# Two-layer decoder trunk on one core: the modulation columns get other stages

## The chip, the core and the metric

The kernel runs on one core of a Trainium2 chip. The core has a matrix engine (TensorE, PE in the profile), a vector engine (VectorE, DVE), an activation engine (ScalarE, ACT), GpSimd (POOL) and a sync engine (SP) that here only issues DMAs. The metric is the device time of one execution in microseconds (us), the median of several runs. Everything is float32, and the matrix products are made of three products each (high by high, high by low, low by high), with each operand split into a rounded high part and the rest.

## The reference

A sequence of 512 tokens with 1024 features passes two layers. Layer 0 mixes tokens by retention, layer 1 by an mLSTM; each has four heads (256 wide for queries and keys, 512 for values) and is followed by a channel mixer with a causal convolution (2816 wide). What the change touches is the conditioning by the vector c:

```python
c_act = jax.nn.silu(c)
for i in range(DEPTH):
    mod = c_act @ ada_w[i] + ada_b[i]
    sh_t, sc_t, gt_t, sh_f, sc_f, gt_f = [m[:, None, :] for m in jnp.split(mod, 6, axis=-1)]
    h = rmsnorm(x, norm_tok_g[i]) * (1.0 + sc_t) + sh_t
    ...
    x = x + gt_t * y
    h = rmsnorm(x, norm_ffn_g[i]) * (1.0 + sc_f) + sh_f
    x = x + gt_f * conv_ffn(h, ffn_w_up[i], ffn_conv_w[i], ffn_conv_b[i], ffn_w_down[i])
return rmsnorm(x, final_g)
```

Each layer's `mod` has 6 times 1024 values: a shift, a scale and a gate for the token mixer and the same for the channel mixer. Features lie on 128 partitions, so a layer has 48 columns of 128 values and the trunk has 96.

## The kernel before

**A modulation column.** Line 456, `side_work`, computes one: SP loads the column's 128 rows of `ada` (1025 floats each, 512.5 KB) into a buffer `ada`, and VectorE multiplies it with the row c and sums along the row (line 452, `gemv`, one SCALAR_TENSOR_TENSOR over 128x1025). For a scale column a tiny instruction makes the gain from it (line 466). The buffers come from a ring of two (`KINDS`, key "a", line 48), so that a third column's load waits until the first one's product has run. The chunks of the down projections (line 510) use the same two buffers.

**When.** 16 columns (the shifts and scales of the first norm) are computed in the opening stage. The other 80 stand in the list `side` in the order of use (lines 1866 to 1874): 8 gates of the first mixer; 16 shifts and scales of the first channel mixer's norm, with its 8 gates behind them; the same 24 for the second layer's token mixer (16 and 8); 16 and 8 for the second channel mixer. `SIDES` (line 30) says how many are taken from the list in which named stage; they are spread evenly over the stage's items (lines 1884 to 1892). An item is a block of matrix products with one chunk of weights. `gate` is the first matmul from that item on: the column's load is not planned to be issued before it. This is an order in the plan and no wait on the chip.

**The stages.** `heads` (line 1295) writes the order of a mixer's four heads out by hand. Stage names are "ret" (retention) or "ml" (mLSTM) with q (queries and keys), v (values), g (gates), o (output projection) and the number of the head, 0 to 3; "o1" projects head 1's output, "o2" the first pieces of head 2's, and "last" the rest beside the coming norm (`boundary`, line 1045). Between them stand scores (S), attention (A) and the ends of heads. The order is q1, v1, g1, (o0), q2, v2, g2, q3, v3, g3, o1, o2, last. Then comes the channel mixer: "up0" or "up1" for its first products, "fold0" or "fold" for the long middle part, where products of the up projection and pieces of the down projection alternate, and "end0" or "end1" for the last group of the down projection beside the next norm. Stage "fold0" hands out its 32 columns by itself (line 891).

**The order on each engine.** `Plan` records every instruction and then orders each engine's own by a simulated run (line 258): an instruction has a price in us (lines 170 to 191), a due time that follows from the matmul which needs its result (lines 241 to 252), and among those that can start soonest the one with the earliest due time goes first. The columns have late due times, so they fill what the simulated VectorE has left over. The list of each engine is then fixed; on the chip an engine takes it strictly in order and waits by semaphore where an operand is missing. The price of a plain DMA is 2.45 us per MB (line 172), of an accumulating one 5.4. The accumulating DMAs are issued by POOL and make the low parts of weights (line 483); all weights are loaded by SP, on the same queue as the columns.

**PE's order** follows the items, with neighbours that interleave. The names of PE's outputs tell the stages: `p` (products of folded pairs, in q, g and fold), `pv` (values), `psc` (scores), `pav` (attention), `po` (output and down projections), `pf` and `pp` (products right behind a norm).

Of the kernel before, what the change touches and what calls it, by code (L numbers as in the profile page):

```python
# [26 lines left out]
GROUPS = [4, 4, 4, 4, 6]  # L27
WCOLS = 1024
WTILES = 18
SIDES = [('ret q1', 4), ('ret v1', 2), ('ret g1', 2), ('ret v3', 6), ('ret g3', 10), ('fold0', 32), ('ml v3', 4), ('ml g3', 8), ('ml o1', 4), ('up1', 8)]  # L30
O_ADDED = (2, 3)
FREE_STEPS = (0, 3)
VADDED = (1, 6, 5, 7, 3)
# [346 lines left out]
def trunk(ctx: ExitStack, tc: tile.TileContext, xT, cb, pos, vec, ident, decay, zmask, ada, w_s0, w_in0, w_v0,  # L380
# [957 lines left out]
    class Ffn:  # L1338
# [75 lines left out]
        def items(self, norm):  # L1414
# [4 lines left out]
            steps, run = folded(folds, self.h, self.start.sums.terms, pairs, downs,  # L1419
                                dict(SIDES).get(f"fold{self.layer}", 0))  # L1420
            now[0] = f"up{self.layer}"
# [456 lines left out]
    for n, (uses, fn, free) in enumerate(items):  # L1878
# [5 lines left out]
        same = [m for m, (used, _, _) in enumerate(items) if steps_at[m] == steps_at[n] and used]  # L1884
        quota = dict(SIDES).get(steps_at[n], 0)
        if not quota or n not in same:
# [121 lines left out]
```

## Time and profile before

| | |
|---|---|
| median of 3 runs | 1508.07 us (1507.39 to 1513.26) |
| the profiled execution | 1507.64 us |
| its span, first to last instruction | 1505.8 us |
| columns, bytes of each | 96, 512.5 KB |
| mean granted clock of TensorE | 0.993 |

Where the stages lie in the span, by the names of PE's outputs and counts of its matmuls (us): ret q1 87.5 to 126.8, v1 to 150.7, g1 to 177.5, o0 to 199.4, q2 to 221.0, v2 to 243.0, g2 to 270.3, q3 to 291.0, v3 to 310.5, g3 to 337.0, o1 to 367.2, o2 to 378.0, last with the norm to 435.0, up0 to 457.0, fold0 to 718.5, end0 to 752.0, the norm and head 0 of ml to 825.0, ml q1 to 854.3, v1 to 878.4, g1 to 907.5, o0 to 929.5, q2 to 951.0, v2 to 973.6, g2 to 1001.8, q3 to 1024.5, v3 to 1043.1, g3 to 1072.0, o1 to 1099.0, o2 to 1110.0, last with the norm to 1174.5, up1 to 1196.3, then the second fold and the end. Neighbouring stages interleave by some us.

A row of the view by stretches gives a stretch of the span (start and end, its length), then the busy time of PE, of PE's weight loads, of DVE, ACT and POOL with the number of instructions, then the granted clock of TensorE (1.00 is full), the mean busy share of the 16 DMA engines (it can pass 1 a little, as packets are counted where they start) and the GB/s that they moved. The stretch's length less PE's busy time is PE's idle time. In the timeline a bracket at the end gives the engine's idle time before the instruction and what ended it.

### The profile page before, as it was taken

To read this page: it belongs to the slowest core of one execution; us is meant where nothing else is said; L and a number is where in the kernel's file an instruction comes from. 1 tells how busy PE (TensorE), PEld (TensorE's weight loads), DVE (VectorE), ACT (ScalarE), POOL (GpSimd) and SP (SyncE) were. 2 spreads that over 40 slices of the span, in tenths; PEclk is the share of its full clock that TensorE was granted. 3 is DMA by queue.
4 is the path that set the end of the run, shared out by engine and by line. 5 is a ranking of instruction groups with operands and counts; after the bars stand their busy time and mean duration, and the time that the engine had idled before them with its cause. 6 is when DMAs were issued, how large, how long until landed. Compare 5 with 4: busy or idle time off the path is not lost.

```text
span 1505.8 us, 27268 instructions
## 1 busy us (share of the span) xinstructions
PE 1472.7 (98%) x10477; PEld 1375.8 (91%) x10477; DVE 1268.1 (84%) x2141; ACT 1070.0 (71%) x1601; POOL 283.5 (19%) x311
## 2 busy tenths in 40 slices
PE   9999999999999999999999999998999999999997
PEld 6889999988999989999989998998989989999997
DVE  6998979498988888898887987888989887777786
ACT  4558868776587676776679985998747867766752
POOL 0234232322011111110001322131211111111100
PEclk9989999999999999999999999999999999999999
DMA  9567978898688989999358866889796888876841
GB/s 362 173 161 191 278 172 215 213 298 233 183 222 210 269 224 273 264 250 270 106 158 194 193 188 141 192 199 225 237 288 161 224 235 215 205 194 166 199 132 57
DMA packets 92980, 315.00 MB, mean 209 GB/s; under 512 B 12193, under 2 KB 14625, under 8 KB 92850
## 3 DMA queue, kind: packets, MB, share of 16 engines
q0 software_dynamic: 31824, 115.88, 41.7%
q1 hardware_dynamic: 61026, 197.38, 36.9%
q8 instruction: 82, 1.34, 0.3%
q14 instruction: 48, 0.39, 0.1%
HBM read 195.23 MB, written 2.12 MB: 131 GB/s over the span
## 4 chain that ended last, share of the span: by engine, by line
PE 85%; DVE 6%; DMA 5%; ACT 2%; issue 2%; POOL 0%; SPq 0%; DVEq 0%; POOLq 0%; ACTq 0%
PE p L376 34%; PE po L376 24%; PE pv L376 7%; PE pp L376 5%; PE pav L376 4%; PE pf L376 4%; PE pst L376 3%; PE psc L376 2%; DMA ada<-ada 1%; DMA wlo<-ws 1%; DMA wb<-w_in 1%; PE pc L376 1%; ACT whi L376 1%; DVE ada L376 1%; DMA wb<-w_up 1%
## 5 line engine op out<-in xcount | busy, mean ns | idle before, releaser
L376 PE MATMUL p<-hh,whi 128*128 128x256 f32 (+1 forms) x994 | 276.3, 278 | 4.4 <-DVE mc L376 4.3
L376 PE MATMUL p<-hl,whi 128*128 128x256 f32 x992 | 276.0, 278 | 0.6 <-DVE hl L376 0.5
L376 PE MATMUL p<-hh,wlo 128*128 128x256 f32 x992 | 273.9, 278 | 0.0
L376 ACT ACTIVATE wlo<-whi 128x1024 fp32r<-128x1024 f32 x221 | 233.1, 1060 | 49.9 <-PE po L376 19.3
L376 PEld LDWEIGHTS p<-hh,whi 128*128 128x128 f32 x994 | 188.1, 189 | 5.3 <-DVE mc L376 4.5
L376 PEld LDWEIGHTS p<-hl,whi 128*128 128x128 f32 x992 | 187.8, 189 | 1.4 <-DVE hl L376 1.1
L376 PEld LDWEIGHTS p<-hh,wlo 128*128 128x128 f32 x992 | 187.0, 189 | 0.1
L376 PE MATMUL p<-t24h,whi 128*128 128x256 f32 x744 | 166.1, 280 | 5.1 <-DVE p L376 3.6
L376 PE MATMUL po<-ggh,wlo 128*128 128x512 f32 (+1 forms) x448 | 153.0, 343 | 1.1 <-DVE wlo L376 1.1
L376 PE MATMUL po<-ggh,whi 128*128 128x512 f32 (+1 forms) x448 | 152.5, 343 | 1.4 <-ACT whi L376 1.4
L376 PE MATMUL po<-ggl,whi 128*128 128x512 f32 (+1 forms) x448 | 153.2, 343 | 0.0
L376 DVE SCALAR_TENSOR_TENSOR x<-po,mod,x 128x512 f32<-128x512 f32 (+1 forms) x184 | 112.0, 625 | 37.7 <-PE po L376 37.2
L376 ACT CAST whi<-raw 128x1024 fp32r<-128x1024 f32 (+1 forms) x117 | 117.5, 1018 | 32.2 <-PE po L376 9.5
L376 PE MATMUL p<-t24l,whi 128*128 128x256 f32 x496 | 138.0, 278 | 0.0
L376 PEld LDWEIGHTS p<-t24h,whi 128*128 128x128 f32 x744 | 127.1, 189 | 8.3 <-DVE p L376 4.7
L376 DVE SCALAR_TENSOR_TENSOR ada<-ada,c_ext 128x1025 f32<-128x1025 f32 x96 | 121.5, 1268 | 9.8 <-DMA ada<-ada 9.7
L376 POOL DMA_DIRECT2D wlo<-wa x62 | 54.6, 880 | 382.2 <-ACT wlo L376 260.7
L376 PE MATMUL po<-yh,whi 128*128 128x256 f32 (+1 forms) x354 | 116.4, 330 | 0.6 <-DVE x L376 0.6
L376 PE MATMUL po<-yl,whi 128*128 128x256 f32 (+1 forms) x352 | 116.3, 330 | 0.3 <-DVE yl L376 0.2
L376 PE MATMUL po<-yh,wlo 128*128 128x256 f32 (+1 forms) x352 | 115.1, 329 | 0.0
L376 DVE SCALAR_TENSOR_TENSOR cv<-p,vecs,cv 128x510 f32<-128x510 f32 (+1 forms) x144 | 105.8, 742 | 7.5 <-ACT cv L376 7.2
L376 ACT CAST whi<-ws 128x1024 fp32r<-128x1024 f32 x86 | 90.2, 1051 | 28.4 <-DVE ws L376 18.7
(285 smaller groups left out, 4428.5 us busy)
## 6 DMA issues: line engine op xcount, KB each, us to landing
ada<-ada SPq DMA_DIRECT2D x96, 512.5 KB, 6.4
wlo<-ws POOLq DMA_DIRECT2D x73, 512.0 KB, 6.9
wlo<-wa POOLq DMA_DIRECT2D x62, 512.0 KB, 6.9
wlo<-wt POOLq DMA_DIRECT2D x44, 512.0 KB, 6.7
wlo<-raw POOLq DMA_DIRECT2D x36, 512.0 KB, 8.8
wa<-w_up SPq DMA_DIRECT2D x36, 512.0 KB, 6.8
wb<-w_up SPq DMA_DIRECT2D x36, 512.0 KB, 6.9
raw<-w_o SPq DMA_DIRECT2D x32, 512.0 KB, 8.8
```

Of the source, the lines that this page charges most:

```text
L376: getattr(c.obj, c.name)(*[real(v) for v in c.a], **{key: real(v) for key, v in c.k.items()})
```

## The change

The list `SIDES` gets other stages and numbers; the 80 columns keep their order, and nothing else changes.

```diff
-SIDES = [('ret q1', 4), ('ret v1', 2), ('ret g1', 2), ('ret v3', 6), ('ret g3', 10), ('fold0', 32), ('ml v3', 4), ('ml g3', 8), ('ml o1', 4), ('up1', 8)]
+SIDES = [("ret q1", 2), ("ret v1", 4), ("ret g1", 4), ("ret g2", 2), ("ret q3", 2), ("ret g3", 3), ("ret o1", 4), ("ret o2", 4), ("fold0", 32), ("end0", 2), ("ml q1", 1), ("ml v1", 4), ("ml g2", 2), ("ml g3", 6), ("ml o2", 4), ("up1", 4)]
```

By stage, the number of columns before and after:

| stage | before | after | | stage | before | after |
|---|---|---|---|---|---|---|
| ret q1 | 4 | 2 | | end0 | 0 | 2 |
| ret v1 | 2 | 4 | | ml q1 | 0 | 1 |
| ret g1 | 2 | 4 | | ml v1 | 0 | 4 |
| ret g2 | 0 | 2 | | ml g2 | 0 | 2 |
| ret q3 | 0 | 2 | | ml v3 | 4 | 0 |
| ret v3 | 6 | 0 | | ml g3 | 8 | 6 |
| ret g3 | 10 | 3 | | ml o1 | 4 | 0 |
| ret o1 | 0 | 4 | | ml o2 | 0 | 4 |
| ret o2 | 0 | 4 | | up1 | 8 | 4 |
| fold0 | 32 | 32 | | sum | 80 | 80 |

Since the plan is made by the simulated run over all instructions, other instructions can change their place in an engine's order too.

## The prediction

> **What bounds the kernel now.** I read the page first, then the busy times by stretch, the waits, the timelines of SP and VectorE where PE stood still, and the chain of waits there.
>
> ```profile
> PE 1472.7 (98%) x10477; PEld 1375.8 (91%) x10477; DVE 1268.1 (84%) x2141; ACT 1070.0 (71%) x1601; POOL 283.5 (19%) x311
> q0 software_dynamic: 31824, 115.88, 41.7%
> q1 hardware_dynamic: 61026, 197.38, 36.9%
> L376 DVE SCALAR_TENSOR_TENSOR ada<-ada,c_ext 128x1025 f32<-128x1025 f32 x96 | 121.5, 1268 | 9.8 <-DMA ada<-ada 9.7
> ```
>
> PE is the bound: of the span's 1505.8 us it is idle for 33.1. The change touches none of its matmuls, so it can only win or lose idle time and clock. One column costs VectorE 1.27 us. On the DMA engines, SP's queue moved 197.38 MB in 36.9% of 1505.8 = 555.6 us, 2.81 us per MB, so a column of 0.525 MB takes 1.48 us of all 16 engines. POOL's accumulating queue takes 41.7% of 1505.8 / 115.88 = 5.42 us per MB, 2.84 us for a tile of 0.524 MB. Now the stretches where PE loses time:
>
> ```profile
> 87.50:126.80 39.30, 36.47 (x241) 34.43 (x240) 36.08 (x60) 24.95 (x40) 13.49 (x14) 0.87 0.52 135
> 291.00:310.50 19.50, 19.11 (x163) 18.75 (x163) 12.66 (x21) 13.40 (x20) 5.80 (x6) 1.00 1.00 263
> 310.50:337.00 26.50, 24.19 (x195) 23.19 (x194) 24.99 (x35) 20.01 (x33) 8.29 (x12) 1.00 1.01 307
> 457.00:718.50 261.50, 260.17 (x1896) 243.62 (x1896) 231.57 (x392) 180.57 (x254) 34.52 (x40) 1.00 0.91 250
> 1024.50:1043.10 18.60, 18.31 (x153) 17.92 (x152) 15.90 (x25) 17.82 (x26) 2.58 (x3) 1.00 1.04 258
> 1043.10:1072.00 28.90, 24.57 (x191) 24.11 (x190) 23.97 (x38) 20.23 (x32) 3.00 (x5) 0.94 0.85 244
> 1099.00:1110.00 11.00, 9.97 (x44) 7.95 (x43) 8.67 (x14) 4.72 (x6) 2.98 (x3) 1.00 1.04 331
> 1110.00:1151.60 41.60, 40.64 (x315) 38.55 (x314) 40.35 (x81) 24.66 (x42) 5.18 (x6) 1.00 0.66 175
> 1196.30:1245.00 48.70, 45.75 (x349) 43.15 (x348) 40.57 (x68) 31.95 (x45) 5.83 (x7) 1.00 0.86 227
> ```
>
> Length less PE's busy time gives PE's idle time: 2.83 us in ret q1, 0.39 in ret v3, 2.31 in ret g3, 1.33 in all of fold0, 0.29 in ml v3, 4.33 in ml g3, 1.03 and 0.96 beside the last heads of ml, 2.95 where the second fold begins. In ml g3 the clock is 0.94 too, which is 0.06 x 28.9 = 1.7 us of PE's time. All of these but ret q1 and fold0 are stages from which columns go. The stages next to the fourth heads have DMA shares of 1.00 to 1.04: there the DMA engines are full.
>
> **The change part by part: what goes.** 29 of the 80 columns change stage. Most expensive is ml v3, 4 columns before and none after:
>
> ```profile
> 1025.06 2.62 SPq L376 DMA_DIRECT2D ada<-ada  x2
> 1029.51 14.82 DMA wb<-w_in
> 1044.46 0.69 DVE L376 TENSOR_TENSOR ws<-wb 128x512 f32<-128x512 f32 x1 [2.25 <-DMA wb<-w_in]
> PE p L376 <- DVE mc L376: 4.3, 1, 4.3
> 1047.70:1051.20 3.50, 3.41 (x16) 3.41 (x17) 3.50 (x7) 2.29 (x5) 0.86 (x1) 0.52 0.91 251
> ```
>
> The first row is SP's queue, the second the chain of waits. Two columns stand on SP ahead of the weights `wb` of ml g3. The weights land 14.82 us after their issue, VectorE stands idle 2.25 us for them, and behind `ws` in VectorE's order stands the convolution tap `mc`, which frees the PSUM bank that PE wants: 4.3 us of idle PE, then a clock of 0.52 for about 3.5 us. Without the two columns the DMA engines have 2 x 1.48 = 2.96 us less to move before `wb`, more than VectorE's 2.25. So `ws` and `mc` come 2.25 us earlier and PE's stall shrinks to 2.1. Below it, what is late next is VectorE's own queue. I count the 1.7 us of clock as gone too: **4.0 us**, between 0 (if `wb` waits for its buffer rather than for the engines) and 0.29 + 4.33 + 1.7 = 6.3.
>
> ```profile
> 95.00:106.00 11.00, 9.23 (x39) 8.55 (x40) 11.00 (x19) 8.03 (x12) 7.26 (x6) 0.53 0.47 117
> PE p L376 <- DVE p L376: 3.6, 4, 1.3
> 1228.79 0.39 PE L376 MATMUL p<-t3h,whi 128*128 128x256 f32 x1 [1.52 <-ACT fs L376]
> ```
>
> Whether the clock falls at 2.1 us is open: a stall of 1.52 us at the second fold left it at 1.00 (row 1196.30), 4.33 did not, and in ret q1 several stalls of at most 1.3 us, 2.83 together, led to 0.53. I take the nearer single stall, 1.52; by ret q1's row the sum below would be 1.7 us worse. [...]
>
> Ret v3 and g3 had 16 columns and keep 3. The first two rows are of columns alone, in the two stretches together: ten instructions, two a column, so five products, and seven loads.
>
> ```profile
> 291.00:337.00 46.00, 7.61 (x10) 1.00 1.01 288
> ada<-ada SPq DMA_DIRECT2D x7, 512.5 KB, 7.9
> 319.66 2.77 DVE L376 SCALAR_TENSOR_TENSOR ada<-ada,c_ext 128x1025 f32<-128x1025 f32 x1
> 1103.41 1.23 DVE L376 SCALAR_TENSOR_TENSOR ada<-ada,c_ext 128x1025 f32<-128x1025 f32 x1 [1.78 <-DMA ada<-ada]
> 1220.62 1.23 DVE L376 SCALAR_TENSOR_TENSOR ada<-ada,c_ext 128x1025 f32<-128x1025 f32 x1 [1.14 <-DMA ada<-ada]
> 1223.79 1.23 DVE L376 SCALAR_TENSOR_TENSOR ada<-ada,c_ext 128x1025 f32<-128x1025 f32 x1 [1.94 <-DMA ada<-ada]
> ```
>
> VectorE is busy 24.99 of 26.5 us in g3, and the product at 319.66, stretched to 2.77 us, lies in the chain ahead of the sums that PE waits for. Two columns fewer there and four loads fewer on full DMA engines (5.9 us) end most of the 0.39 + 2.31 = 2.70 us: **2.0**, between 0 and 2.7.
>
> The end of ml (g3 8 to 6, o1 4 to 0, o2 0 to 4): at 1103.41 VectorE idles 1.78 us for a column and then computes it, with the normalisation of the last head behind it. The columns that remain there are gates of the last channel mixer, needed only in the second fold, so the plan need not press them in: **1.5** of 1.99, between 0 and 2.0. Up1 (8 to 4): at 1220.62 and 1223.79 VectorE idles 1.14 + 1.94 us for columns and computes for 2.46, and PE's stalls follow at 1228.79. Counted back from the trunk's last product they are the fifth and sixth of the stage's eight; with four they are not there: **2.5** of 2.95, between 0 and 2.95.
>
> ```profile
> 65.70:125.00 59.30, 0.00 (x0) 0.91 0.47 115
> ```
>
> Ret q1 (4 to 2) is worth **nothing**: by this row of columns alone no product of one runs there before 125 us, and VectorE is busy 36.08 of 39.3 us with the opening's own work.
>
> The sum of what goes is 4.0 + 2.0 + 1.5 + 2.5 = 10.0 us, at most 14.0.
>
> **What is added.** The places:
>
> ```profile
> 126.80:150.70 23.90, 23.90 (x197) 23.55 (x196) 19.98 (x32) 21.01 (x37) 12.56 (x14) 1.00 0.96 251
> 150.70:177.50 26.80, 26.80 (x217) 26.27 (x216) 25.20 (x41) 24.52 (x41) 3.00 (x5) 1.00 0.98 293
> 243.00:270.30 27.30, 27.30 (x219) 26.78 (x218) 20.21 (x37) 23.78 (x39) 6.66 (x10) 1.00 0.89 227
> 270.30:291.00 20.70, 20.70 (x179) 20.70 (x178) 11.79 (x17) 17.25 (x27) 7.35 (x7) 1.00 0.83 185
> 337.00:367.20 30.20, 30.20 (x149) 25.52 (x148) 24.77 (x44) 21.37 (x33) 6.04 (x6) 1.00 0.81 213
> 367.20:378.00 10.80, 10.80 (x49) 8.97 (x48) 9.23 (x12) 7.11 (x8) 2.57 (x3) 1.00 1.05 293
> 718.50:752.00 33.50, 33.50 (x294) 33.50 (x293) 26.02 (x53) 20.90 (x36) 3.46 (x4) 1.00 0.36 101
> 825.00:854.30 29.30, 29.30 (x226) 28.43 (x225) 27.48 (x47) 28.64 (x46) 7.62 (x11) 1.00 0.82 198
> 854.30:878.40 24.10, 24.10 (x197) 23.72 (x196) 22.86 (x35) 20.99 (x36) 9.41 (x9) 1.00 0.67 143
> 878.40:907.50 29.10, 27.81 (x221) 26.96 (x220) 24.85 (x39) 25.74 (x42) 5.37 (x8) 1.00 0.82 229
> 973.60:1001.80 28.20, 27.74 (x220) 26.88 (x219) 25.51 (x43) 26.22 (x43) 7.38 (x11) 1.00 0.85 192
> 125.00:177.50 52.50, 8.12 (x12) 1.00 0.97 273
> ```
>
> The last row is of columns alone: six ran in ret v1 and g1 (two instructions each) and PE lost nothing. Ret g2 and q3 have 7.1 + 8.9 us of VectorE free for 4 x 1.27 = 5.1, and 0.11 x 27.3 + 0.17 x 20.7 = 6.5 us of DMA for 5.9. Ret o1 and o2 get columns that ran there anyway, as late ones of g3. End0 has 7.5 us free for 2.5. Tightest is ml v1: with q1's, five columns want 6.35 us, v1 has 1.24 free and g1, where PE already loses 1.29, has 4.25, so about one spills into o0. I price an added column as one of fold0, where 32 ran and PE lost 1.33: 0.04 us, 29 x 0.04 = **1.2**. Its bounds are 0 and what columns cost where they stood badly: 14.0 in all.
>
> A column's issue that waits for one of the two buffers holds SP, and the weights behind it. The two issues at 1025.06 took 2.62 instead of 2 x 0.33 us, so a hold is about 2.0. Weights of the next item stand behind it; the lead of the loads hides it except where DMA shares are near 1.
>
> Together: 1507.64 (the profiled execution, 1.84 above its span) - 10.0 + 1.2 = 1498.8, and as the median of before lies 0.43 above that execution, I say **1499**.
>
> **The rivals.** *The stalls move along* (0.25): each column costs in its new place what it cost in the old. With half of the 14.0 us given back it is 1507.6 - 14.0 + 7.0 = 1500.6, with all of it 1507.6; I take 1504, from 1501 to 1509. For it: ml v1 and g1 have little of VectorE free. Against it: six columns without loss in ret v1 and g1, 32 nearly so in fold0.
>
> *All four stalls go and nothing comes* (0.12): 1507.6 - 14.0 = 1493.6. For it speaks that what holds PE is a column's load or product in each; against it that VectorE stays over 0.9 busy in those stretches.
>
> *Columns ahead of weights where the DMA engines are full* (0.13), the slower side: the plan prices a column at 0.525 x 2.45 + 0.05 = 1.34 us of DMA and the trace at 1.48. Two columns more in ret v1 and g1 want 2.96 us where 0.04 x 23.9 + 0.02 x 26.8 = 1.5 are free; four in g2 and q3 leave 0.6; o2 is at 1.05. If weights then come late by more than VectorE's lead, each place pays as ml g3 did, 4.33 + 1.7 = 6.0: three places are 18, 1498.8 + 18 = 1516.8. It decides from the third place on; with one or two it ends within 1511. Against it: PE idles nowhere in those five stretches today. [...]
>
> **How the numbers follow.** The forecast itself gets 0.50, with a range of its own of 1495 to 1503, which the bounds of the four terms and of the clock make; about 0.36 of it lies below 1500.5. A measurement of this kernel can tell about 0.5% from no change, 7.5 us. So faster by more is 0.36 + 0.12 = 0.48, slower by more 0.13, and the rest 0.39. The range leaves out the tip of the second rival and most of the slower one: 1492 to 1511.
>
> **What would show it.** Right: in ml g3 PE's idle time falls from 4.33 to about 2 and the clock returns to 1.00; in the second fold's beginning VectorE no longer waits for columns and PE idles under 0.5; in ret g3 PE idles under 0.7; ret q1 still idles 2.8 at 0.87. Wrong: PE idle over 1 us in ret v1 to q3 or ml v1 and g1, weights that land after 14 us there, or VectorE's order changed so that other work is late in the old places.

## The result and the profile after

The changed kernel takes **1497.14 us** (median of 6 runs, 1494.54 to 1498.65). Beside it, the kernel before took 1508.74 (6 runs, 1507.39 to 1513.26). The ratio is 0.9918, with a 95% interval from 0.9902 to 0.9934. So the change saves about 0.8%, or 11.6 us. The prediction said 1499, which is 1.9 us too high.

The profiled execution took 1497.61 us, with a span of 1495.8 and a mean clock of 0.995. That is 10.0 us less than the profiled execution of before in both numbers. First the page of the changed kernel, its line of busy times:

```profile
PE 1468.1 (98%) x10477; PEld 1373.1 (92%) x10477; DVE 1264.9 (85%) x2141; ACT 1069.4 (71%) x1601; POOL 285.3 (19%) x311
```

PE's idle time is 1495.8 - 1468.1 = 27.7 us where it was 33.1, so 5.4 of the 10.0 us were idle time. The other 4.6 went from its busy time (1472.7 to 1468.1), though the matmuls are the same: a matmul lasts longer at half clock (16 of them fill a stretch in which 32 run at full clock, in rows shown further down). Between 50 and 1460 us, half clock lasted 10.24 + 3.41 us before and 6.83 after, which is about 3.4 of the 4.6; where the rest lies was not looked into. Next the busy times by stretch, in the stages from which columns went. They have the columns explained above: stretch, length, PE, PEld, DVE, ACT, POOL, clock, DMA share, GB/s.

```profile
87.40:126.40 39.00, 34.97 (x242) 33.18 (x241) 36.13 (x60) 25.12 (x40) 13.47 (x14) 0.91 0.52 135
291.00:310.40 19.40, 19.40 (x168) 19.31 (x167) 14.11 (x21) 14.04 (x19) 4.47 (x5) 1.00 1.05 261
310.40:336.00 25.60, 24.05 (x195) 23.55 (x194) 18.57 (x27) 18.18 (x32) 5.39 (x10) 1.00 0.96 304
455.00:718.00 263.00, 259.79 (x1887) 242.61 (x1886) 229.46 (x387) 180.66 (x254) 34.46 (x40) 1.00 0.92 247
1026.00:1044.70 18.70, 18.70 (x159) 18.59 (x159) 17.00 (x27) 18.01 (x26) 6.81 (x6) 1.00 0.97 222
1044.70:1070.00 25.30, 23.40 (x194) 22.90 (x194) 20.87 (x31) 20.62 (x34) 2.13 (x4) 1.00 0.95 287
1096.00:1146.50 50.50, 50.30 (x363) 46.63 (x362) 45.22 (x85) 29.15 (x47) 7.42 (x9) 1.00 0.77 203
1191.20:1240.00 48.80, 48.80 (x371) 46.31 (x370) 41.89 (x70) 35.59 (x50) 6.88 (x8) 1.00 0.85 215
```

Read length less PE's busy time, and then the clock. In ml g3 (1044.70) the idle time fell from 4.33 to 1.90 us, and the clock is 1.00 again. The second fold's beginning (1191.20) has no idle time left, where it had 2.95. Ret g3 (310.40) has 1.55 instead of 2.31. But fold0 (455.00), whose 32 columns were not touched, rose from 1.33 to 3.21.

Now stretches that got columns:

```profile
126.40:150.20 23.80, 23.80 (x196) 23.49 (x195) 23.31 (x33) 21.58 (x37) 11.02 (x14) 1.00 0.98 235
150.20:177.30 27.10, 27.10 (x217) 26.55 (x216) 24.91 (x40) 23.87 (x41) 2.84 (x4) 1.00 0.91 274
270.00:291.00 21.00, 21.00 (x181) 21.00 (x180) 11.37 (x18) 18.09 (x29) 10.20 (x9) 1.00 0.90 211
855.60:880.00 24.40, 24.40 (x199) 23.97 (x198) 21.11 (x35) 20.51 (x33) 9.54 (x9) 1.00 0.89 207
```

PE is busy all the time in each of them, in ret v1 even with VectorE busy for 23.31 of 23.80 us. So in this execution the columns left no idle time there.

Idle time alone hides the clock and small delays. So I also added up, over all of PE's matmuls, how much later each one starts after the one before it than is usual (the median) for its shape. This is called **lost time** below; it holds the idle time and the time lost to half clock. It was 55.1 us before and is 45.1 after, again 10.0 us less. By place (own sums from the two traces, us, the differences taken before rounding):

| place in the span | before | after | difference |
|---|---|---|---|
| 80-120, ret q1 | 8.7 | 8.4 | -0.3 |
| 120-280, ret v1 to q3 | 2.8 | 3.5 | +0.7 |
| 280-340, ret v3 and g3 | 4.7 | 3.1 | -1.6 |
| 460-720, fold0 | 2.2 | 4.8 | +2.6 |
| 720-940, end0 to ml o0 | 5.6 | 6.2 | +0.5 |
| 940-1020, ml q2 to q3 | 2.3 | 3.7 | +1.3 |
| 1020-1080, ml v3 and g3 | 7.8 | 3.3 | -4.5 |
| 1080-1200, end of ml, up1 | 5.7 | 2.5 | -3.2 |
| 1200-1280, second fold's beginning | 5.0 | 0.1 | -4.9 |
| the rest | 10.4 | 9.8 | -0.6 |

The stages from which columns went gave 1.6 + 4.5 + 3.2 + 4.9 = 14.2 us, and 0.7 + 2.6 + 0.5 + 1.3 = 5.1 came back elsewhere. So by these two executions the small net gain is a large gain, partly given back. How far a single execution can be trusted in one place is said under the experiments.

What happened in ml g3 is in the timelines of SP, of VectorE and of PE:

```profile
1032.94 0.33 SPq L376 DMA_DIRECT2D wb<-w_in  x1
```
```profile
1038.52 0.74 DVE L376 SCALAR_TENSOR_TENSOR mc<-p,vecs,mc 128x509 f32<-128x509 f32 x1
1040.53 0.69 DVE L376 TENSOR_TENSOR ws<-wb 128x512 f32<-128x512 f32 x1 [0.50 <-DMA wb<-w_in]
```
```profile
1059.19 0.38 PE L376 MATMUL p<-t24h,wlo 128*128 128x256 f32 x1 [1.90 <-DMA wlo<-ws]
```

Two things differ from before. The weights `wb` are there at 1040.53, at most 7.6 us after their issue instead of 14.82. And the plan has put the tap `mc` **ahead of** the sum `ws` in VectorE's order: it ran at 1038.52, two microseconds before the weights that had held it up. The 4.33-us stall is gone altogether. The 1.90 us that the stretch still shows is another stall, for the low half of a weight that POOL's accumulating queue brings.

### The profile page after: what moved, and what is told of

Its sections match the earlier page's. It is cut to its first block, busy times and chain, and to the rows that moved or that the text cites. A ratio compares the mean times of both kernels' runs of the same rounds, so it can differ in the third digit from the quotient of the medians.

```text
span 1495.8 us, 27226 instructions
## 1 busy us (share of the span) xinstructions
PE 1468.1 (98%) x10477; PEld 1373.1 (92%) x10477; DVE 1264.9 (85%) x2141; ACT 1069.4 (71%) x1601; POOL 285.3 (19%) x311
## 4 chain that ended last, share of the span: by engine, by line
PE 81%; DMA 7%; DVE 6%; issue 2%; ACT 2%; POOL 1%; DVEq 0%; POOLq 0%; SPq 0%; ACTq 0%
PE p L376 34%; PE po L376 23%; PE pv L376 7%; PE pp L376 5%; PE pf L376 4%; PE pav L376 3%; DMA wb<-w_up 2%; PE psc L376 2%; PE pst L376 2%; DMA wlo<-ws 2%; DMA ada<-ada 1%; DVE ada L376 1%; ACT whi L376 1%; DVE wlo L376 1%; DVE ws L376 1%
## 5 line engine op out<-in xcount | busy, mean ns | idle before, releaser
L376 DVE SCALAR_TENSOR_TENSOR cv<-p,vecs,cv 128x511 f32<-128x511 f32 (+1 forms) x144 | 106.2, 743 | 7.5 <-ACT cv L376 7.2
```

What stands on the lines that cost most here:

```text
L376: getattr(c.obj, c.name)(*[real(v) for v in c.a], **{key: real(v) for key, v in c.k.items()})
```

## The experiments

Twelve kernels ran. Each ratio is to the kernel before, timed beside it on the same chip, with its 95% interval. Lost time is that of one profiled execution of each.

How much it varies can be read where two kernels have the same columns and the same order of instructions on every engine (by their traces). Fold0 lost 0.7 to 2.2 us in the five that share it with before (before, v3_only, up1_only, ml_only, tap_first). Ret v1 to q3 lost 3.5 to 5.1 us in the four that share it with the changed kernel (that one, ret_only, fold_shift, fold24). Ml v3 and g3 lost 7.6 to 10.5 us in three (before, up1_only, ret_only), and the second fold's beginning 3.8 to 6.5 us in three (before, ret_only, tap_first). So a difference of 1.5 us in one place, and in some places of close to 3, shows nothing by itself. In the table above, the gains from 1020 us on, the gain in ret v3 and g3, and the losses in fold0 and from ml q2 to q3 stand outside what such executions show; the +0.5 from 720 to 940 does not.

### What the columns themselves cost

A column is a load on the DMA engines and a product on VectorE. The order of all instructions was left as planned, and only the size of what was issued was cut: the load to 128 of 1025 floats, or the product to 16 of 1025 elements, or both.

```diff
-        S.dma_start(raw, ada[layer, f]).after = gate
-        gemv(layer, f, raw)
+        load = S.dma_start(raw, ada[layer, f])
+        load.after = gate
+        product = gemv(layer, f, raw)
+        load.short = raw[:, :128], ada[layer, f][:, :128]
+        product.short = raw[:, :16], c_ext[:, :16], 1e-3, c_ext[:, :16]
...
-            getattr(c.obj, c.name)(*[real(v) for v in c.a], **{key: real(v) for key, v in c.k.items()})
+            getattr(c.obj, c.name)(*[real(v) for v in c.short or c.a], **{key: real(v) for key, v in c.k.items()})
```

This is b_both; a_both has the same edit with the stages of the changed kernel; b_load has full-width products that do not read the load; b_prod has full loads.

> The kernel before with its order and its waits on every engine kept, but the 80 side columns almost free: a load brings 128 of 1025 floats of each row and a product runs over 16 elements instead of 1025, on c alone (so the modulations are not the reference's). Theory: the time of before over after (11.6 us) is what loads and products cost in their old places, so this comes out at 1491 to 1497 us, with PE's stalls gone in ret g3, ml g3, the end of ml and the start of the second fold. Rival: the gain came from another order of the other instructions, which the plan made around the columns; then this stays at 1504 to 1509 us.

> As the one with almost free columns, but the products keep their full width of 1025 elements; only the loads are an eighth (the products run on c alone). Theory that the loads are the main price (full DMA engines in ml v3, VectorE waiting for columns at the end of ml and in the second fold): 1497 to 1501 us. Theory that VectorE's products are: 1504 to 1508 us.

> The kernel before with full loads, but products over 16 of the 1025 elements (the modulations are sums over 16). If the loads are the main price: 1503 to 1507 us, with the stall of 4.3 us in ml g3 still there and the one in ret g3 gone. If the products are: 1496 to 1501 us.

> The changed kernel with its order and waits kept and almost free columns (loads an eighth, products over 16 elements, on c alone). It tells what the columns still cost in their new places. Theory by the sum of the prediction (29 moved columns at 0.04 us, some 4 us left in the old places and fold0): 1492 to 1496 us. Rival that the stalls moved along in part: 1486 to 1491 us.

| kernel | median, us | before, us | ratio (95%) | lost time, us |
|---|---|---|---|---|
| b_load | 1497.14 | 1507.09 | 0.9936 (0.9922 to 0.9949) | 44.6 |
| b_prod | 1503.32 | 1507.09 | 0.9975 (0.9964 to 0.9986) | 50.5 |
| b_both | 1493.13 | 1507.09 | 0.9909 (0.9895 to 0.9923) | 42.1 |
| a_both | 1490.22 | 1507.09 | 0.9886 (0.9871 to 0.9901) | 37.3 |

In before's order the loads cost 9.95 us and the products 3.77, and both together 13.96: the two costs add up, within the intervals. The loads are the larger part, though the rows in which PE waits name VectorE and ScalarE for the most part. Nearly free columns are worth 13.96 us in before's order; the changed order, with columns in full, got 11.6. Beside a_both, which has the changed kernel's order, the columns still cost the changed kernel some 5 to 7 us: 6.9 by the medians, and 0.9918 - 0.9886 = 0.0032 of 1507 = 4.8 by the ratios. That lies in the range that was given for stalls that moved along in part (1486 to 1491 us).

The four kernels also split the gain. b_both and a_both have the same nearly free columns and differ in places and order alone: 2.9 us by the medians, 3.5 by the ratios, with intervals that just overlap. So of the 11.6 us some 3 are another order of the rest, and the larger part is that the columns themselves cost 5 to 7 us instead of 14.

The stall in ml g3 shows what a load is and what an order is. In b_load, the two short columns still stand on SP ahead of `wb`. First its VectorE, then its PE:

```profile
1039.72 0.68 DVE L377 TENSOR_TENSOR ws<-wb 128x512 f32<-128x512 f32 x1
...
1042.25 0.74 DVE L377 SCALAR_TENSOR_TENSOR mc<-p,vecs,mc 128x509 f32<-128x509 f32 x1
```
```profile
1043.05 0.39 PE L377 MATMUL p<-hh,whi 128*128 128x256 f32 x1 [2.30 <-DVE mc L377]
```

No bracket stands at `ws` now: the weights come in time, and VectorE goes without a pause from `ws` to `mc`. PE still waits 2.30 us, for VectorE's own queue of four sums ahead of the tap. The prediction expected 2.1 from this. In the changed kernel it was the new order that took away the rest.

### The parts of the change one by one

v3_only moves the four columns of ml v3 to ml v1. up1_only moves four of up1's eight to ml o2. ret_only takes over the change in the first layer's mixer; ml_only takes over all behind fold0. One column less in ret o2, and one more in ml g3, hold the sum at 80. The edits in `SIDES`, in this order:

```diff
-('ml v3', 4), ('ml g3', 8),
+('ml v1', 4), ('ml g3', 8),
```
```diff
-('ml o1', 4), ('up1', 8)]
+('ml o1', 4), ('ml o2', 4), ('up1', 4)]
```
```diff
-('ret q1', 4), ('ret v1', 2), ('ret g1', 2), ('ret v3', 6), ('ret g3', 10),
+('ret q1', 2), ('ret v1', 4), ('ret g1', 4), ('ret g2', 2), ('ret q3', 2), ('ret g3', 3), ('ret o1', 4), ('ret o2', 3),
```
```diff
-('ml v3', 4), ('ml g3', 8), ('ml o1', 4), ('up1', 8)]
+('end0', 2), ('ml q1', 1), ('ml v1', 4), ('ml g2', 2), ('ml g3', 7), ('ml o2', 4), ('up1', 4)]
```

> Before, with the 4 columns of ml v3 moved to ml v1 and nothing else. The step of the prediction: two loads ahead of the weights are the cause, 4.0 us with the clock, so 4 us under before and a stall of about 2 us left in ml g3 (the run with short loads had 2.3 us and the clock still fell). Rival: the plan's new order of VectorE (the convolution tap no longer behind the late weights) takes the stall away altogether, 5 to 6.5 us under before.

> Before, with 4 of up1's 8 columns moved to ml o2 and nothing else. The prediction's term: 2.5 us under before, at most 2.95. By PE's lost time in the two traces (4.4 us less between 1200 and 1270 us): 3 to 4.5 us under before. If the stall only moves to the end of ml, where o2's four columns come on top of o1's: within 1 us.

> Before the middle part as changed (but ret o2 3, so that the second layer starts on the column it started on before), everything from ml on as before. By the prediction's terms: 2.0 us less for ret v3 and g3, 0.5 more for what is added, so 1.5 us under before. By PE's lost time in the two traces (2.1 us less in ret g3, but 2.9 more within fold0): 0.8 over before, if fold0's new stalls come from the columns of the first layer.

> The first layer's mixer as before, everything from end0 on as changed (but ml g3 7, to hold the sum). By the prediction's terms: 4.0 + 1.5 + 2.5 - 0.7 = 7.3 us under before. By PE's lost time in the two traces from 1020 us on: about 10 to 11 us under before.

| kernel | median, us | before, us | ratio (95%) | lost time, us |
|---|---|---|---|---|
| v3_only | 1497.98 | 1506.39 | 0.9948 (0.9935 to 0.9961) | 44.9 |
| up1_only | 1505.51 | 1506.99 | 0.9995 (0.9983 to 1.0007) | 53.1 |
| ret_only | 1505.07 | 1506.39 | 0.9991 (0.9980 to 1.0002) | 55.1 |
| ml_only | 1491.86 | 1506.39 | 0.9912 (0.9898 to 0.9926) | 42.1 |

**v3_only** saves 7.8 us by its ratio, twice the term of 4.0. But in ml v3 and g3 itself its lost time fell by 5.3 us (7.8 to 2.5), little more than the term. The rest lies where the edit moved nothing: the end of ml and up1 went from 5.7 to 2.4, fold0 from 2.2 to 0.7, 720 to 940 from 5.6 to 4.1, while 940 to 1020 and the second fold rose by 1.0 and 0.8. Up to 848 us, where SP issues the first moved load, the order of every engine is that of before, so fold0's part is a difference between two executions. Behind it the plan wrote another order: in ml g3 the tap stands ahead of three of the four sums and PE does not wait for it, so this run does not part the loads from the order. At the end of ml the order is another one too, and 3.3 us went there without a column being moved.

**up1_only** does exactly what the prediction said in its own place: the second fold's beginning went from 5.0 us lost to 0.0. And it pays that back 70 us earlier, where the end of ml and up1 went from 5.7 to 9.2. SP, VectorE and PE of up1_only, then two stretches:

```profile
1125.70 12.74 SPq L376 DMA_DIRECT2D ada<-ada  x4
```
```profile
1154.19 1.23 DVE L376 SCALAR_TENSOR_TENSOR ada<-ada,c_ext 128x1025 f32<-128x1025 f32 x1 [1.57 <-DMA ada<-ada]
...
1155.34 0.48 DVE L376 SCALAR_TENSOR_TENSOR hl<-xr,mod,hh 128x256 fp32r<-128x256 f32 x1
```
```profile
1155.87 0.39 PE L376 MATMUL pf<-hl,whi 128*128 128x256 f32 x1 [2.03 <-DVE hl L376]
```
```profile
1153.60:1157.01 3.41, 1.38 (x7) 0.96 (x8) 2.82 (x7) 1.30 (x3) 0.86 (x1) 1.00 1.06 262
1157.01:1160.42 3.41, 3.41 (x16) 3.14 (x16) 3.41 (x7) 2.72 (x5) 0.00 (x0) 0.50 1.00 359
```

With ml o1's four columns still there, the four in ml o2 come on top. SP is held 12.74 us by four columns' issues, VectorE waits 1.57 us for a column, and behind that product in its order stands `hl`, the normalised input that PE wants. PE waits 2.03 us and then runs at half clock for 3.41 us. In the changed kernel ml o1's four had been taken away too; ml_only, with o1's four gone too, lost 1.2 and 0.1 us in the two places. Taking o1's four away alone was not tried.

**ret_only** cannot be told from no change. Its trace shows the gain in its place (4.7 to 3.2 in ret v3 and g3) and the price beside it (2.8 to 5.0 in ret v1 to q3). Part of that price is this stall in ret g1, the first row below; fold_shift and fold24 have it too, with 0.80 and 0.56 us. The changed kernel has the same order there, and its profiled execution shows no stall at this place.

```profile
167.94 0.38 PE L376 MATMUL p<-t3h,whi 128*128 128x256 f32 x1 [0.96 <-ACT fs L376]
1048.38 0.58 PE L376 MATMUL p<-hh,whi 128*128 128x256 f32 x1 [4.99 <-DVE mc L376]
```

In ml g3, where nothing was moved, it lost 10.5 us instead of 7.8 (the second row, 4.99 instead of 4.33 us of stall, and two stretches of half clock instead of one). From 700 us on the order of every engine is that of before, so this is a difference between two executions and no effect of the edit.

**ml_only** saves 13.3 us by its ratio, as much as the whole change (the two intervals overlap, 0.9898 to 0.9926 and 0.9902 to 0.9934). So the change in the first layer's mixer adds nothing that could be measured.

### One instruction out of the way

tap_first is the kernel before with all columns where they were. In VectorE's finished order, one instruction stands elsewhere: the tap `mc` of ml g3 ahead of the four sums `ws`, `ws`, `wt`, `wt`.

```diff
-        for n in self.order():
+        order = self.order()
...
+        order.remove(tap)
+        order.insert(order.index(first), tap)
...
+        for n in order:
```

> The kernel before with its columns where they were; one VectorE instruction is moved, the last convolution tap that frees the PSUM bank PE waits for in ml g3: it goes ahead of the four sums of folded weights (ws, ws, wt, wt) that wait for the late load, instead of behind them. If the late load does harm only through VectorE's strict order: PE's stall of 4.3 us and the half clock behind it are gone, 5 to 6.5 us under before, although the weights land as late as before. If the late weights themselves are what PE needs (the prediction's step, by loads): within 2 us of before, with the stall a little later.

It took 1506.18 us beside 1506.99, a ratio of 0.9990 (0.9979 to 1.0000): at most 3.2 us, where 5 to 6.5 had been expected if the late load did harm through VectorE's order alone. Its VectorE, its ScalarE, its PE, and then its stretches:

```profile
1043.86 0.74 DVE L387 SCALAR_TENSOR_TENSOR mc<-p,vecs,mc 128x509 f32<-128x509 f32 x1
1046.19 0.69 DVE L387 TENSOR_TENSOR ws<-wb 128x512 f32<-128x512 f32 x1 [1.59 <-DMA wb<-w_in]
```
```profile
1047.64 1.05 ACT L387 CAST whi<-ws 128x1024 fp32r<-128x1024 f32 x1 [2.36 <-DVE ws L387]
...
1051.16 0.35 ACT L387 COPY fs<-p 128x256 f32<-128x256 f32 x1
```
```profile
1051.56 0.38 PE L387 MATMUL p<-t24h,whi 128*128 128x256 f32 x1 [3.06 <-ACT fs L387]
```
```profile
1046.41:1049.82 3.41, 2.09 (x19) 1.89 (x17) 3.38 (x5) 2.15 (x3) 0.00 (x0) 1.00 1.05 187
1049.82:1053.24 3.42, 1.68 (x14) 1.68 (x15) 3.42 (x10) 3.42 (x6) 0.86 (x1) 1.00 0.91 247
1053.24:1056.65 3.41, 3.41 (x32) 3.41 (x31) 1.99 (x5) 3.38 (x7) 0.86 (x1) 1.00 1.03 254
```

The tap is early and PE gets its bank. A few matmuls later it waits 3.06 us for `fs`, a copy on ScalarE. That copy stands behind the casts of the late weights, and the first of those casts waited 2.36 us for the same `ws`. So the late weights hold PE by a second engine when the first is freed. The clock stays at 1.00, which saves the halving, and the place lost 6.3 us instead of 7.8; the second fold lost 6.5 in this trace instead of 5.0, in the same order. Of the 4.33 us of stall, 3.06 are left without the tap's place and 2.30 (b_load) without the late load; in the changed kernel both are gone, and so is the stall.

### Looking for a better version

fold_shift and fold24 are the changed kernel with one column, or eight, moved to end0; mix28 is ml_only with four columns moved from fold0 to end0.

```diff
-("ret o2", 4), ("fold0", 32), ("end0", 2),
+('ret o2', 3), ('fold0', 32), ('end0', 3),
```
```diff
-("fold0", 32), ("end0", 2),
+('fold0', 24), ('end0', 10),
```
```diff
-('fold0', 32), ('end0', 2),
+('fold0', 28), ('end0', 6),
```

> The changed kernel with ret o2 3 and end0 3, so that fold0 hands out the same columns as before. If fold0's new stalls of PE (at 544, 614, 636 and 667 us, 3.2 idle together against 1.3 before) come from the shift by one column: 2 to 3 us under the changed kernel, with at most 1.3 us idle in fold0. If they are chance or come from the loads' phase: within 1 us of the changed kernel.

> The changed kernel with 24 columns in fold0 instead of 32 and 10 in end0 instead of 2. With almost free columns the changed kernel lost nothing in fold0, with full ones 4.6 us there; if a quarter fewer columns take that away and end0 (7.5 us of VectorE free) hides the eight: 3 to 4 us under the changed kernel, 1493 us. If the place of a column in the plan counts more than their number: anywhere from 1491 to 1502 us.

> The first layer's mixer as before, fold0 28 and end0 6, the rest as in the run that changed the second layer alone (ml q1 1, v1 4, g2 2, g3 7, o2 4, up1 4), which was 14.5 us under before. If number counts: 1 to 2 us under that run. If the place in the plan counts: up to 6 us over it.

| kernel | median, us | before, us | ratio (95%) | lost time, us |
|---|---|---|---|---|
| fold_shift | 1503.95 | 1506.39 | 0.9983 (0.9973 to 0.9994) | 48.5 |
| fold24 | 1501.80 | 1506.99 | 0.9968 (0.9957 to 0.9978) | 48.5 |
| mix28 | 1495.79 | 1506.99 | 0.9924 (0.9909 to 0.9940) | 43.2 |

None is shown to beat the changed kernel, and neither is ml_only, at 0.9912 beside 0.9918. In fold0 all three did what was meant: 4.8 us lost in the changed kernel, and 1.1, 0.1 and 1.0 in these (0.7 to 2.2 in before's order). But from 720 to 940 fold_shift lost 11.2 us and fold24 15.0, where the changed kernel lost 6.2. The cause of the largest piece can be read from POOL's timeline. First the changed kernel's, then that of fold24, its PE and its stretches:

```profile
871.22 0.86 POOL L376 DMA_DIRECT2D wlo<-wa  x1 [6.59 <-ACT fs L376]
872.74 3.11 POOL L376 TENSOR_TENSOR zv<-zq,zq 128x512 f32<-128x512 f32 x2 [0.66 <-ACT zq L376]
```
```profile
871.91 3.00 POOL L376 TENSOR_TENSOR zv<-zq,zq 128x512 f32<-128x512 f32 x2 [7.75 <-ACT zq L376]
874.86 0.86 POOL L376 DMA_DIRECT2D wlo<-wt  x1
879.15 0.86 POOL L376 DMA_DIRECT2D wlo<-wa  x1 [3.44 <-ACT wlo L376]
```
```profile
888.96 0.58 PE L376 MATMUL p<-hh,wlo 128*128 128x256 f32 x1 [3.13 <-DMA wlo<-wa]
```
```profile
884.42:887.83 3.41, 1.40 (x13) 1.21 (x11) 3.41 (x8) 3.41 (x6) 0.86 (x1) 1.00 1.04 273
887.83:891.24 3.41, 2.28 (x10) 2.29 (x11) 0.80 (x2) 0.80 (x3) 1.07 (x2) 0.50 1.06 308
```

In the changed kernel POOL issues the low half of the weight `wa` at 871.22, ahead of its products `zv`. In fold24 it comes behind them, at 879.15; PE stands 3.13 us for it and falls to half clock. fold_shift shows the same order and a stall of 2.24 us at that place. Neither edit moves a column to ml v1 or g1: a column that is put elsewhere in one stage changes the simulated run, and with it POOL's order over 100 us later. Why the plan then chose so was not looked into.

## Why the prediction was right or wrong, point by point

The time was right within 2 us, but that is in part luck: by the two traces, two errors of about the same size in the working cancel. The terms that go were 10.0 us and came out at about 14; the price of what is added was 1.2 and came out at about 5. Each is a sum over single executions, so both are good to some us; that the columns still cost 5 to 7 us in all is shown by a_both as well.

- **ml v3 and g3, 4.0 us: right in size, half right in how.** The place gave 4.5, alone (v3_only) 5.3. That two loads make `wb` late, and that VectorE's queue is late next, is shown by b_load: no wait at `ws`, and a stall of 2.30 us against 2.1. In the changed kernel the plan also put the tap ahead, which the prediction did not foresee, and `wb` came 7.2 us sooner after its issue instead of 2.96.
- **The clock at a stall of 2.1 us: wrong.** The step took the nearer single stall, 1.52 us, which had kept the clock. In b_load 2.30 us halved it, and 3.06 us in tap_first did not: the length of one stall does not decide (see the last section). In the changed kernel that stall is gone, and its clock in ml g3 is 1.00.
- **Ret v3 and g3, 2.0 us: right in place (1.6), but given back.** Alone it is worth nothing that can be told from zero. PE idles 1.55 us in g3, not the 0.7 that was named as the sign.
- **The end of ml, 1.5 us: too small (3.2 with up1), and not for the reason given.** VectorE waits for a column still, and longer (1.78 us before):

```profile
1101.53 1.23 DVE L376 SCALAR_TENSOR_TENSOR ada<-ada,c_ext 128x1025 f32<-128x1025 f32 x1 [3.19 <-DMA ada<-ada]
```

  PE has work in that time: it idles 0.20 us in the stretch from 1096.00. What made the difference was not settled; v3_only lost no more there (2.4 us) with all columns of g3, o1 and up1 in their old places.
- **Up1, 2.5 us: too small (4.9).** The columns that held VectorE are gone, as said. The step counted only the idle time up to 1245; small delays and the stalls from there to 1280 went too. up1_only shows the condition that the step left out: the four columns that ml o2 gets must not meet the four of ml o1.
- **Ret q1, nothing: right** (-0.3 us), though the sign named for it, 2.8 us idle at 0.87, did not come: it idled 4.03 us at 0.91, with 6.83 us of half clock instead of 10.24.
- **What is added, 1.2 us: too small by 3.9, and in other places.** Where columns were added in ret v1, g1, q3, o2 and ml v1, PE idles nowhere in the profiled execution, and under 1 us in ret g1 in the three others of the same order. In two of these, ret_only and fold_shift, a stall near 210 us brings the sum from ret v1 to q3 to 1.8 and 2.1 us, over the 1 us that was named as a sign of being wrong; these stalls name `fs` and VectorE's `p`, none a load. So the third rival, columns ahead of weights at 6 us a place, is not what these four executions show. The loss came in fold0 (+2.6), which the prediction had taken as its yardstick for cheap columns, and from ml q2 to q3 (+1.3). The first is these two stalls of the changed kernel, behind ScalarE's `fs`:

```profile
545.09 0.39 PE L376 MATMUL p<-t24h,whi 128*128 128x256 f32 x1 [1.05 <-ACT fs L376]
668.67 0.38 PE L376 MATMUL p<-t24h,whi 128*128 128x256 f32 x1 [1.78 <-ACT fs L376]
```

  a_both runs the same order with nearly free columns and loses 0.1 us in fold0: there it is the columns' own work. From 940 to 1020 it loses 3.7 us like the changed kernel: there it is the order.
- **The rivals.** "The stalls move along" was to give back half of what goes; 5.1 of 14.2 us is somewhat less than that, so what happened lies between it and the forecast, though the time does not (1497 is below both). "All four stalls go and nothing comes" was right in its first half, as the old places gave their bound of 14, and wrong in its second. The mechanism of the third rival, a late weight of 2 to 3 us and then the clock, is what fold_shift and fold24 show at one place each, by POOL's order and not by columns ahead on SP.

## What to carry to other kernels

When a scheduler writes the order, an edit of what fills the gaps is also an edit of every engine's order: compare the orders first (here a tap on VectorE, a weight load on POOL). One column put elsewhere in fold_shift made the changed kernel 7 us slower by the medians, with a new stall through POOL's order. Judge a part of such a change by an experiment that keeps the order and shrinks the work, and one that changes a single stage; a part that is worth nothing alone (up1_only) can be worth something beside others (ml_only, which has it, gained 5.5 us more than v3_only). Before a difference in one place is read from two traces, look for two traces of the same order and see how far they differ there. And where a late transfer and an instruction that is queued behind it make a stall, take away both: either alone left more than half of it here (3.06 and 2.30 of 4.33 us).

## What the hardware showed that was not expected

**Half clock came and went on a grid of 3.41 us, and followed the lost time summed over one stretch of it.** All changes of the granted clock lie on such a grid in each trace, and half clock lasted one, two or three stretches of it (3.41 us in ml g3 and 10.24 in ret q1 before, 6.83 in ret q1 after). In the fourteen profiles between 50 and 1460 us, I added PE's lost time in each stretch at full clock (delays over 0.1 us): all 23 with 2.15 us or more were followed by half clock, and no stretch with 2.00 or less was (own sums from the traces; the kernel before has 3.33 and 2.20 ahead of half clock and next 2.00, at 1225.37, the changed kernel 2.15 and next 1.82). The stretch before each clock change and the one behind it, from the kernel before (two places, then the stretch from 1225.37, behind which the clock stays) and then the changed kernel in ret q1:

```profile
92.09:95.50 3.41, 1.93 (x13) 1.32 (x11) 3.41 (x9) 2.90 (x6) 0.00 (x0) 1.00 0.74 233
95.50:98.91 3.41, 2.92 (x11) 2.33 (x11) 3.41 (x8) 2.45 (x6) 1.45 (x2) 0.51 0.00 0
1044.48:1047.89 3.41, 0.10 (x1) 0.10 (x1) 3.38 (x6) 1.95 (x2) 0.00 (x0) 1.00 1.08 195
1047.89:1051.30 3.41, 3.41 (x16) 3.41 (x17) 3.40 (x7) 2.20 (x5) 0.86 (x1) 0.50 0.90 254
1225.37:1228.78 3.41, 1.84 (x14) 1.44 (x13) 3.41 (x8) 3.04 (x4) 0.68 (x1) 1.00 1.02 339
```
```profile
94.90:98.30 3.40, 1.81 (x11) 1.41 (x11) 3.40 (x9) 2.73 (x5) 1.09 (x1) 1.00 0.07 28
98.30:101.72 3.42, 2.07 (x9) 2.07 (x10) 3.42 (x7) 2.98 (x5) 3.28 (x4) 0.51 0.29 98
```

This answers what the prediction left open. Several short stalls of ret q1 fall into one stretch (13 matmuls in 3.41 us, where before's stretch from 88.68 has 32; 2.20 us lost), and a clock of 0.51 follows. A stall of 3.06 us in tap_first falls on two stretches, which lose 1.44 and 1.89 us, and the clock stays at 1.00. In b_load a stall of 2.30 us, with small delays beside it in the same stretch, loses 2.59, and 0.51 follows. By these sums, 3.06 us inside one stretch would have been over 2.15, so for a stall near this size it counts how it lies on the grid; this is an estimate, as no run shifts a stall alone.

**Loads of one size land at very different times after their issue.** The same 0.5 MB of `wb` were there 7.6 us after their issue at the latest in the changed kernel, and 14.82 us after it in the kernel before, with two columns of 0.525 MB ahead of them in the same queue; by before's own rate of 1.48 us a column that would be 2.96 us. b_load has the two columns in the same places of the queue with an eighth of the bytes: there the last of the 16 updates of `wb`'s semaphore came 10.64 us after its issue. So the columns' bytes account for some 4.2 us, more than their own rate gives, and about 3 us remain between that order and the changed one. What these were, POOL's accumulating transfers or the place in the queue, was not tried apart.
